# Rotated queries by SBUF copies, and two weight casts queued behind the exponentials, in a hybrid attention block

## The chip, the cores and the metric

The kernel runs on one core of a Trainium2 chip. The metric is the device time of one launch in microseconds (us). Three runs of the kernel before gave 628.59, 629.05 and 629.34 us; the median is 629.05.

## The reference

One decoder block over 512 tokens of width 1024, with 16 learned meta tokens in front (528 positions). Two attention branches of 16 heads each run side by side: MLA (queries and keys from low-rank projections, with a rotated part of 32 dimensions per head) and FoX (plain heads with a cumulative forget gate added to the logits). Both are gated, projected back and merged:

```python
u = rmsnorm(h, pre_norm_g)
cq, ckv, k_pe, z_mla, fq, fk, fv, f_logit, z_fox, gate_a, gate_b = split(u @ w_in)
q_m = concat(q_nope, rope(q_pe))          # from rmsnorm(cq) @ w_uq, per head 64 + 32
k_m = concat(k_nope, rope(k_pe))          # from rmsnorm(ckv) @ w_ukv; rope(k_pe) shared by the heads
o_mla = softmax(causal(q_m @ k_m.T * s)) @ v_mla
o_fox = softmax(causal(fq @ fk.T * s + cum_t - cum_s)) @ fv
y_mla = (o_mla * silu(z_mla)) @ w_br_mla ;  y_fox = (o_fox * silu(z_fox)) @ w_br_fox
out = h + rmsnorm((sigmoid(gate_a) * y_mla + sigmoid(gate_b) * y_fox) @ w_out)
```

All inputs and outputs are float32.

## The kernel before

Every float32 operand of a matmul is halved into a rounded part and a rest (`h` and `l` in the names: `wh`/`wl` for weights, `uTh`/`uTl` for activations), and each product is three matmuls: high by high, low by high, high by low. A block of weights of 128 columns is loaded as 512 KB into `wraw` (a pool of three buffers), cast to `wh` by ScalarE (ACT, line 126) and subtracted to `wl` by GpSimd (POOL, line 127 through the helper at line 101). A `unit` (line 171) is the list of matmul steps of one such block; its first step fetches the weights and issues the loads of the three blocks behind it.

After a front part (normalisation, transposition, small projections) come sixteen attention stages, for each pair of heads first FoX, then MLA: the first stage is FoX of pair 0, the second MLA of pair 0, the third FoX of pair 1. TensorE (PE) has an order written out by hand: in every stage the scores of the first three query blocks (`s0`, tile `st`), the value product of the stage before (`late`, tile `ov`, whose transposed probabilities are `pt`), the scores of the last query block (`s1`), and then the `fill`: projections that the next stages need. The second stage's fill is the projections of FoX pair 1: queries `fq`, half of the keys `fk`, values `v`, the other half of `fk`. A projection's result stands in one of three PSUM accumulators until ACT (`hlq`, `hlk`, line 238) and VectorE (DVE, line 101) have halved it; the second half of `v` needs the accumulator of `fq`.

The softmax of a stage: DVE masks and takes the minimum (line 642, `sf`), ACT takes the exponentials (line 650, six for the first three blocks of two heads, two for the last block), DVE sums and inverts (lines 658, 659, `su` and `ri`), POOL, ACT and DVE normalise into float16 halves `pn` (lines 664 to 678), and eight transposing DMAs put them into `pts` (tile `pt`, line 683).

The queues of ACT, DVE, POOL and of SyncE (SP), which issues all DMAs, are ordered by a planner that simulates the engines and issues what is ready first by priority. Two things bind it. `dma` (line 87) keeps a DMA in program order while `written[0]` is set, which holds for the first stage. And `wsplit` (line 121) queues its cast behind `behind[0]`, if there is one (`issue_after`: an order on the queue, without a semaphore). `behind` is filled in the first stage with the tanh of MLA's gate `z` (line 595) and cleared at the end of the second (line 788); so in the second stage the casts of `fq`, `fk` and `v` come behind that tanh.

The rotated queries: `pe_unit(0)` (line 483) computes them for heads 0 to 7; `rest` (line 517) adds and halves them on POOL into `rr[x]` (x = the first or second half of the rotation, inside `gT`), with 16 rows to each head, and stores them to `qpe_dram`: heads 0 and 1 at once (line 527, two DMAs for each x), heads 2 to 7 in the second stage (line 774). `load_qp` (line 461) loads the 128 rows of a pair into `QP`, for pair 0 in the first stage (line 763), ahead of that stage's transposes. The MLA scores read `QP`.

Of the kernel before, what the change touches and what calls it, by code (L numbers as in the profile page):

```python
# [16 lines left out]
AF = mybir.ActivationFunctionType  # L17
# [32 lines left out]
def f32(ap):  # L50
    return ap.bitcast(F32)
# [3 lines left out]
def block_kernel(ctx: ExitStack, tc: tile.TileContext, x, meta_tokens, pre_norm_g, w_in, fox_forget_b,  # L55
                 mla_q_norm_g, mla_kv_norm_g, w_uq, w_ukv, w_br_mla, w_br_fox, w_out, post_norm_g,
                 rope_tok, rope_pe, out):
    nc = tc.nc
# [23 lines left out]
    wp = ctx.enter_context(tc.tile_pool(name="wp", bufs=3))  # L82
    uid = [0]
    written = [False]
    behind, through, first_t = [], [], []

    def dma(out, src, start=None):

        ins = (start or nc.sync.dma_start)(out=out, in_=src)
        if written[0]:  # L90
            tc.keep_in_program_order(ins)
        return ins.ins

    def mm(*a, **k):
        nc.tensor.matmul(*a, **k)  # L95
# [4 lines left out]
    def split_lo(eng, lo, src, hi):  # L100
        eng.tensor_tensor(out=lo, in0=src, in1=f32(hi), op=ALU.subtract)  # L101
# [31 lines left out]
    def weights(srcs, wrap):  # L133

        st = {}

        def load():
            if "l" not in st:
                st["l"] = wload(srcs())

        def get():
            load()
            return wrap(wsplit(st["l"]))
        get.load = load
        return get
# [65 lines left out]
    def run(steps):  # L211
        for _, fn in steps:
            fn()
# [46 lines left out]
    with ExitStack() as ph:  # L260
# [30 lines left out]
        for c in range(4):  # L291
            r = pa.tile([128, 2, NSM], F32, tag="wsr", name=f"wsr{c}", bufs=4)
# [132 lines left out]
    with ExitStack() as att:  # L425
# [7 lines left out]
        QP = ac.tile([128, S], F32R, tag="QP", name="QP")  # L433
# [27 lines left out]
        def load_qp(pr):  # L461
            dma(f32(QP), qpe_dram[2 * pr : 2 * pr + 2].rearrange("h i x f s -> (h i x f) s"))
# [20 lines left out]
        def pe_unit(g):  # L483
            if g == 0:
                r0, tt = (p.rearrange("p a b -> p (a b)")[:, 0 : 8 * S].bitcast(F32).rearrange("p (c s) -> p c s", c=4)
                          for p in pts)
            else:
                r0, tt = gT[0][:, 4:8], gT[1][:, 4:8]
            rp = r0[:, 0:2]

            rr = [r0[:, 2:4], tt[:, 2:4]] if g else [t[:, 4:6] for t in gT]
            if g == 0:
                nc.sync.dma_start(rp, rope_pe)
            out = []
            w = {}

            def half(xi, ws=None):
                if ws:
                    w[0] = ws
                return (lambda k: w[0][2 * xi + k][0]), (lambda k: w[0][2 * xi + k][1])  # L500

            def srcs():
                if g:

                    tc.keep_in_program_order(nc.sync.dma_start(rp, rope_pe))
                return [wuqh[:, k, 8 * g : 8 * g + 8, NOPE + 16 * x : NOPE + 16 * x + 16]
                        for x in range(2) for k in range(2)]

            for xi in range(2):
                get = (lambda: half(1)) if xi else weights(srcs, lambda ws: half(0, ws))  # L510

                def done(i, ps, xi=xi):
                    for cs in range(2):
                        nc.vector.tensor_tensor(out=tt[:, 2 * xi + cs], in0=ps, in1=rp[:, cs], op=ALU.mult)
                out += unit(f"ppe{g}{xi}", get, cq_act, 2, REAL, done)

            def rest(x):

                nc.gpsimd.tensor_tensor(out=tt[:, x], in0=tt[:, x], in1=tt[:, 3 - x], op=(ALU.subtract, ALU.add)[x])
                hi, lo = rr[x][:, 0], rr[x][:, 1]  # L520
                nc.gpsimd.tensor_copy(hi.bitcast(F32R), tt[:, x])
                split_lo(nc.gpsimd, lo.bitcast(F32R), tt[:, x], hi)
                if g:
                    store(x, 0, 8)
                else:

                    store(x, 0, 2)

            def store(x, a, b):
                for i in range(2):  # L530
                    dma(qpe_dram[8 * g + a : 8 * g + b, i, x], rr[x][16 * a : 16 * b, i])
            return out, rest, store

        mw = {}
# [64 lines left out]
        def attention(br, pr):  # L599


            scale = (SC_MLA, SC_FOX)[br]
# [3 lines left out]
            def sets(h, b, c0, w):  # L606
                hs = slice(64 * h, 64 * h + 64)
                qs, ks = slice(128 * b, 128 * b + 128), slice(c0, c0 + w)
                out = [(q[hs, i, qs], k[hs, j, ks]) for i, j in ((0, 0), (1, 0), (0, 1))]
                if br:  # L610
                    return out + [(ONE[hs], CT[hs, ks])]
                return out + [(QP[hs, qs], KP[i][hs, ks]) for i in range(2)]

            sums, sfs = {}, {}

            def sf_of(h, b):
                o, n = SF_STEP * (b % 3), 144 + 128 * b
                return sfs[b // 3][:, h, o : o + n]

            def scores(g):  # L620

                banks = (((0, 0, 144, 0), (1, 0, 272, 144)), ((2, 0, 400, 0),)) if g == 0 else \
                    (((3, 0, HALF, 0),), ((3, HALF, L - HALF, 0),))

                def fn():
                    if g == 0:
                        for t in ("nb", "su", "ri"):
                            sums[t] = aw.tile([128, 2, 4], F32, tag=t, name=f"{t}{nm_}")
                    sfs[g] = aw.tile([128, 2, (2 * SF_STEP + 400, L)[g]], F32, tag=f"sf{g}", name=f"sf{nm_}{g}", bufs=1)
                    for ib, parts in enumerate(banks):  # L630
                        ps = [stp.tile([128, 512], F32, tag="st", name=f"st{nm_}{g}{ib}{h}") for h in range(2)]
                        for b, c0, w, o in parts:
                            for i, ops in enumerate(zip(*(sets(h, b, c0, w) for h in range(2)))):
                                for h, (Q, K) in enumerate(ops):
                                    mm(ps[h][:, o : o + w], Q, K, start=(i == 0), stop=(i == 4 - br))
                        for b, c0, w, o in parts:
                            m0 = 384 - 128 * b + c0
                            for h in range(2):
                                nb = sums["nb"][:, h, b : b + 1]

                                with tc.high_priority(offset=100):
                                    nc.vector.tensor_tensor_reduce(  # L642
                                        out=sf_of(h, b)[:, c0 : c0 + w], in0=ps[h][:, o : o + w],
                                        in1=maskt[:, m0 : m0 + w], scale=-scale, scalar=3.0e38 if c0 == 0 else nb,
                                        op0=ALU.add, op1=ALU.min, accum_out=nb)
                    with tc.high_priority(offset=60):
                        for b in GRP[g]:
                            for h in range(2):
                                sf = sf_of(h, b)
                                nc.scalar.activation(sf, sf, AF.Exp, bias=sums["nb"][:, h, b : b + 1], scale=-1.0,  # L650
                                                     accum_out=sums["su"][:, h, b : b + 1])
                return fn

            def norm(g):
# [71 lines left out]
        g = gate_unit()  # L726
# [3 lines left out]
        for si, (br, pr) in enumerate(stages):  # L730
# [10 lines left out]
            else:  # L741
                g = gate_unit()
# [9 lines left out]
        late = []  # L752
        for si, (br, pr) in enumerate(stages):
            s0, s1, n0, n1, va = attention(br, pr)

            for fn in [s0] + late + [s1]:
                fn()

            fill = fills[si]
            if si == 0:  # L760

                run(fill[:4])
                load_qp(0)
                n0()
                n1()
                first_t.extend(through)
                run(fill[4:])
            else:
                run(fill[:1])
                if si == 1:  # L770

                    written[0] = True
                    for x in range(2):
                        store0(x, 2, 8)
                    written[0] = False
                run(fill[1:5])
                n0()
                run(fill[5:12])
                n1()
                if 6 <= si < 8:  # L780

                    written[0] = True
                    rest1(si - 6)
                    written[0] = False
                run(fill[12:])
            written[0] = False
            if si == 1:
                behind.clear()
            late = [va]
# [146 lines left out]
```

## Time and profile before

| | us |
|---|---|
| median of three runs | 629.05 |
| the profiled execution's own time | 628.52 |
| its span, from first to last instruction | 626.7 |
| PE busy, share of the span | 602.4, 96% |
| ACT, DVE, POOL busy | 329.0, 310.4, 266.5 |
| mean granted TensorE clock | 0.996 of full speed |

The lines of the timeline give the start in us from the span's start, the duration in us, the engine, the line of the code, the operation with its output and inputs, the shapes, and how many instructions are merged; in brackets stands how long the engine was idle before it and what ended that. A row of waits names the engine that waited, for whom, and the total, the count and the longest. A row of the windows gives for a stretch the busy time and count of PE, of its weight loads, of DVE, ACT and POOL, and then the granted TensorE clock, the share of the DMA engines and GB/s. SPq is SyncE's queue of DMAs; its durations are times to issue, not to land.

### The profile page before, as it was taken

The page shows a single profiled execution, that of the slowest core. Times are in us where ns is not written, and L with a number is a line of the kernel's source. Part 1 is how long each engine was busy: PE and PEld are TensorE (multiplying, and loading weights), DVE is VectorE, ACT ScalarE, POOL GpSimd, SP SyncE. Part 2 cuts the span into 40 slices and gives each one's busy share as a digit, 9 for nine tenths or more (in the row PEclk, how much of TensorE's full clock was granted, in tenths as well). Part 3 has the DMA queues.
Part 4 walks back from the last instruction along what each step waited for, and adds up shares of the span by engine and source line. Part 5 has one row for each costly group of instructions (what it writes and reads, how often), then busy time and mean ns, then how long its engine had stood idle before and what let it go on. Part 6 is the DMA issues. An engine that isn't in the chain of part 4 may idle for free.

```text
span 626.7 us, 10961 instructions
## 1 busy us (share of the span) xinstructions
PE 602.4 (96%) x3810; PEld 507.7 (81%) x3810; DVE 310.4 (50%) x899; ACT 329.0 (52%) x738; POOL 266.5 (43%) x269
## 2 busy tenths in 40 slices
PE   3999998899999999999999999999999999999996
PEld 2879877788888889789888898887888888888885
DVE  4747753467566655764675666636321122023134
ACT  5747726567665665774685666657322222232321
POOL 3216715434344653444254433441744444444610
PEclk9999999899999999999999999999999999999999
DMA  9432369998978778878579586782433333333702
GB/s 286 106 101 51 73 150 191 210 178 169 183 167 152 166 170 169 193 177 198 126 163 189 136 165 163 171 164 67 135 102 100 88 90 92 100 102 114 256 33 101
DMA packets 223808, 90.10 MB, mean 144 GB/s; under 512 B 141628, under 2 KB 216764, under 8 KB 223752
## 3 DMA queue, kind: packets, MB, share of 16 engines
q1 hardware_dynamic: 223752, 89.39, 60.9%
q8 instruction: 30, 0.49, 0.3%
q14 instruction: 26, 0.21, 0.1%
HBM read 55.21 MB, written 4.26 MB: 95 GB/s over the span
## 4 chain that ended last, share of the span: by engine, by line
PE 86%; DVE 4%; ACT 3%; issue 2%; DMA 2%; SPq 1%; POOL 0%; DVEq 0%; ACTq 0%
PE pg L95 14%; PE py L95 14%; PE z L95 14%; PE v L95 9%; PE fk L95 7%; PE po L95 7%; PE fq L95 7%; PE st L95 4%; PE psm L95 3%; PE ov L95 3%; DVE sf L642 2%; ACT wh L126 2%; PE mq L95 2%; PE mk L95 1%; DMA wsr<-in_w_in_dram 1%
## 5 line engine op out<-in xcount | busy, mean ns | idle before, releaser
L101 POOL TENSOR_TENSOR wl<-wraw,wh 128x1024 fp32r<-128x1024 f32 (+1 forms) x90 | 208.4, 2319 | 223.4 <-ACT wh L126 218.6
L126 ACT CAST wh<-wraw 128x1024 fp32r<-128x1024 f32 (+1 forms) x90 | 89.9, 1001 | 175.4 <-PE v L95 48.5
L650 ACT ACTIVATE sf<-sf,nb 128x144 f32<-128x144 f32 (+3 forms) x128 | 72.0, 564 | 14.9 <-DVE nb L642 14.9
L678 DVE SCALAR_TENSOR_TENSOR pn<-sf,ri,pn 128x128 f16<-128x128 f32 (+3 forms) x128 | 66.0, 554 | 13.2 <-ACT pn L677 13.1
L677 ACT ACTIVATE pn<-sf,ri 128x128 f16<-128x128 f32 (+3 forms) x128 | 61.5, 551 | 19.2 <-ACT sf L650 18.5
L819 DVE SCALAR_TENSOR_TENSOR tb<-th,py 128x512 f32<-128x512 f32 x16 | 11.0, 686 | 101.9 <-PE py L95 101.9
L95 PE MATMUL st<-hlk,hlq 64*128 64x272 f32 (+3 forms) x480 | 52.5, 315 | 1.8 <-ACT hlk L238 0.6
L95 PE MATMUL z<-uTh,wh 128*128 128x512 f32 x128 | 50.9, 397 | 0.0
L95 PE MATMUL pg<-uTh,wh 128*128 128x512 f32 x128 | 50.2, 392 | 0.0
L95 PE MATMUL z<-uTh,wl 128*128 128x512 f32 x128 | 50.0, 391 | 0.0
L95 PE MATMUL z<-uTl,wh 128*128 128x512 f32 x128 | 49.9, 390 | 0.0
L95 PE MATMUL pg<-uTl,wh 128*128 128x512 f32 x128 | 49.8, 389 | 0.0
L95 PE MATMUL pg<-uTh,wl 128*128 128x512 f32 x128 | 49.8, 389 | 0.0
L95 PE MATMUL py<-gh,wl 128*128 128x512 f32 x128 | 49.8, 389 | 0.0
L95 PE MATMUL py<-gh,wh 128*128 128x512 f32 x128 | 49.8, 389 | 0.0
L95 PE MATMUL py<-gl,wh 128*128 128x512 f32 x128 | 49.8, 389 | 0.0
L642 DVE CUSTOM_DVE_ANT_0 sf<-st,maskt 128x272 f32<-128x272 f32 (+2 forms) x128 | 48.3, 433 | 0.8 <-PE st L95 0.8
L664 POOL TENSOR_TENSOR mt<-sf,ri 128x96 f32<-128x96 f32 (+1 forms) x32 | 9.5, 296 | 87.9 <-DVE ri L659 74.1
L95 PEld LDWEIGHTS st<-hlk,hlq 64*128 64x128 f32 x480 | 36.9, 185 | 11.9 <-DVE nb L642 2.7
L95 PE MATMUL v<-uTh,wh 128*128 128x256 f32 (+1 forms) x128 | 37.3, 291 | 3.0 <-DVE hlq L101 3.0
L95 PE MATMUL v<-uTl,wh 128*128 128x256 f32 (+1 forms) x128 | 37.2, 291 | 0.0
L95 PE MATMUL v<-uTh,wl 128*128 128x256 f32 (+1 forms) x128 | 37.1, 290 | 0.0
(182 smaller groups left out, 1404.2 us busy)
## 6 DMA issues: line engine op xcount, KB each, us to landing
wraw<-in_w_in_dram SPq DMA_DIRECT2D x56, 512.0 KB
wraw<-in_w_br_fox_dram SPq DMA_DIRECT2D x8, 512.0 KB
wraw<-in_w_br_mla_dram SPq DMA_DIRECT2D x8, 512.0 KB
wraw<-in_w_out_dram SPq DMA_DIRECT2D x8, 512.0 KB
QP<-qpe_dram SPq DMA_DIRECT2D x8, 256.0 KB
pt<-pn SPq DMA_TRANSPOSE x128
xr<-in_x_dram SPq DMA_DIRECT2D x4, 512.0 KB
out_dram<-yo SPq DMA_DIRECT2D x8, 256.0 KB
```

The lines of the kernel that those rows point to most:

```text
L95: nc.tensor.matmul(*a, **k)
L101: eng.tensor_tensor(out=lo, in0=src, in1=f32(hi), op=ALU.subtract)
L126: nc.scalar.copy(wh[:, :n], raw[:, :n])
L642: nc.vector.tensor_tensor_reduce(out=sf_of(h, b)[:, c0 : c0 + w], in0=ps[h][:, o : o + w], in1=maskt[:, m0 : m0 + w], scale=-scale, scalar ...
L650: nc.scalar.activation(sf, sf, AF.Exp, bias=sums["nb"][:, h, b : b + 1], scale=-1.0, accum_out=sums["su"][:, h, b : b + 1])
L664: nc.gpsimd.tensor_tensor(out=mt, in0=src, in1=ri.unsqueeze(3).broadcast_to([128, 2, nb_, META]), op=ALU.mult)
L677: nc.scalar.activation(hi, sf, AF.Copy, scale=rib)
L678: nc.vector.scalar_tensor_tensor(out=lo, in0=sf, scalar=rib, in1=hi, op0=ALU.mult, op1=ALU.subtract)
L819: nc.vector.scalar_tensor_tensor(out=tb[br], in0=ths[i, br], scalar=1.0, in1=py, op0=ALU.add, op1=ALU.mult)
```

## The change

The first pair's rotated queries no longer go through DRAM. In place of the four stores of heads 0 and 1 and the load of `QP`, `rest` issues eight DMAs from `rr[x]` straight into `QP`, one for each x, head and half, with 16 rows of 512 float32 (32 KB). The later pairs still go by `qpe_dram`.

The casts of weights that the second stage makes after its first fill steps (those of `fk` and `v`; the cast of `fq` is made within these first steps) are queued behind the last exponential of the first three query blocks of that stage, in place of the tanh.

```diff
-    behind, through, first_t = [], [], []
+    behind, through, first_t, exps = [], [], [], []
...
                 else:
-                    store(x, 0, 2)
+                    for h in range(2):
+                        for i in range(2):
+                            r = 64 * h + 32 * i + 16 * x
+                            dma(f32(QP[r : r + 16]), rr[x][16 * h : 16 * h + 16, i])
...
             sums, sfs = {}, {}
+            exps[:] = [None, None]
...
-                                nc.scalar.activation(sf, sf, AF.Exp, bias=sums["nb"][:, h, b : b + 1], scale=-1.0,
-                                                     accum_out=sums["su"][:, h, b : b + 1])
+                                exps[g] = nc.scalar.activation(sf, sf, AF.Exp, bias=sums["nb"][:, h, b : b + 1],
+                                                               scale=-1.0, accum_out=sums["su"][:, h, b : b + 1]).ins
...
             if si == 0:
                 run(fill[:4])
-                load_qp(0)
                 n0()
                 n1()
...
                 run(fill[1:5])
+                if si == 1:
+                    behind[:] = exps[:1]
                 n0()
                 run(fill[5:12])
```

## The prediction, on record before the result

> **What bounds the kernel now.** I read the page first, then who waits for whom on the engine that the page shows full, then the timeline of that engine where it waits, and from there the queues of the engines that it waits for.
>
> ```profile
> span 626.7 us, 10961 instructions
> PE 602.4 (96%) x3810; PEld 507.7 (81%) x3810; DVE 310.4 (50%) x899; ACT 329.0 (52%) x738; POOL 266.5 (43%) x269
> ```
> ```profile
> PE v L95 <- DVE hlq L101: 3.0, 1, 3.0
> ```
> TensorE (PE) is busy for 96% of the span, so only its stalls can be won. The longest one after the front stages is this single event. PE's timeline shows it, and smaller ones before it, all within the second attention stage (the brackets give the idle time before the row and what ended it).
>
> ```profile
> 88.87 0.56 PE L95 MATMUL st<-hlk,hlq 64*128 64x144 f32 x6
> ...
> 92.35 2.01 PE L95 MATMUL ov<-pt,vp 80*64 80x512 f16 x25 [0.78 <-DMA pt<-pn]
> ...
> 95.94 0.50 PE L95 MATMUL fq<-uTh,wh 128*128 128x512 f32 x1 [0.16 <-ACT wh L126]
> ...
> 98.37 0.50 PE L95 MATMUL fq<-uTh,wl 128*128 128x512 f32 x1 [1.69 <-POOL wl L101]
> ...
> 112.57 0.39 PE L95 MATMUL v<-uTh,wh 128*128 128x256 f32 x1 [2.99 <-DVE hlq L101]
> ...
> 120.00 0.56 PE L95 MATMUL st<-hlk,hlq 64*128 64x144 f32 x6
> ...
> 122.38 2.04 PE L95 MATMUL ov<-pt,vp 80*64 80x512 f16 x26
> ```
> ```profile
> 139.53 0.56 PE L95 MATMUL st<-hlk,hlq 64*128 64x144 f32 x6
> ...
> 145.65 0.50 PE L95 MATMUL fq<-uTh,wh 128*128 128x512 f32 x1
> ...
> 162.99 0.56 PE L95 MATMUL st<-hlk,hlq 64*128 64x144 f32 x6
> ```
> A stage runs from its first score matmul (st) to the next stage's. The second takes 120.00 - 88.87 = 31.13 us. The fourth, which has the same matmuls, takes 162.99 - 139.53 = 23.46 us. The difference, 7.67 us, is all that can be won here. It is more than the stalls, because after the 2.99 us stall the clock falls:
>
> ```profile
> 113.40:117.00 3.60, 3.60 (x20) 3.60 (x19) 0.00 (x0) 0.00 (x0) 0.36 (x1) 0.53 1.32 188
> 89.00:120.00 31.00, 25.37 (x196) 22.52 (x197) 14.13 (x48) 16.31 (x39) 12.93 (x14) 0.94 0.98 191
> ```
> The granted clock is 0.53 for 3.60 us, which loses 3.60 x 0.47 = 1.7 us. Together with 0.78 + 0.16 + 1.69 + 2.99 that is 7.3; the rest is restarts.
>
> Now the queue that feeds these stalls, SyncE's (SP):
>
> ```profile
> 68.41 2.24 SPq L89 DMA_TRANSPOSE vp<-vh  x1
> ...
> 71.51 2.70 SPq L89 DMA_DIRECT2D qpe_dram<-gT  x4
> 79.55 0.36 SPq L89 DMA_DIRECT2D QP<-qpe_dram  x1
> 80.01 10.59 SPq L89 DMA_TRANSPOSE pt<-pn  x8
> 91.06 1.98 SPq L89 DMA_DIRECT2D wraw<-in_w_in_dram  x3
> ...
> 94.96 2.63 SPq L89 DMA_TRANSPOSE vp<-vh  x1
> 97.64 3.97 SPq L89 DMA_DIRECT2D qpe_dram<-gT  x4
> 101.72 1.82 SPq L89 DMA_DIRECT2D wraw<-in_w_in_dram  x1
> ...
> 111.74 8.08 SPq L89 DMA_TRANSPOSE pt<-pn  x5
> ```
> The four stores are issued by 74.21. Then SP stands until 79.55, 5.34 us, because the load of QP needs them landed. Queued behind are the eight transposes (until 90.60) and the three loads at 91.06, the weights of fq, fk and v.
>
> ```profile
> 94.84 1.05 ACT L126 CAST wh<-wraw 128x1024 fp32r<-128x1024 f32 x1 [4.45 <-DMA wraw<-in_w_in_dram]
> ...
> 99.00 1.05 ACT L126 CAST wh<-wraw 128x1024 fp32r<-128x1024 f32 x1 [0.34 <-DMA wraw<-in_w_in_dram]
> 99.95 0.41 ACT L650 ACTIVATE sf<-sf,nb 128x144 f32<-128x144 f32 x1
> ...
> 111.22 0.57 ACT L238 CAST hlq<-fq 128x512 fp32r<-128x512 f32 x1
> ```
> ```profile
> 76.23 3.04 DVE L678 SCALAR_TENSOR_TENSOR pn<-sf,ri,pn 128x256 f16<-128x256 f32 x5 [0.50 <-ACT pn L677]
> ...
> 92.89 0.57 DVE L642 CUSTOM_DVE_ANT_0 sf<-st,maskt 128x400 f32<-128x400 f32 x1
> ...
> 103.12 0.39 DVE L658 TENSOR_SCALAR su<-su 128x6 f32<-128x6 f32 x1 [9.65 <-ACT sf L650]
> ...
> 111.82 0.69 DVE L101 TENSOR_TENSOR hlq<-fq,hlq 128x512 fp32r<-128x512 f32 x1 [0.61 <-ACT hlq L238]
> ```
> ```profile
> 95.97 2.34 POOL L101 TENSOR_TENSOR wl<-wraw,wh 128x1024 fp32r<-128x1024 f32 x1 [7.02 <-ACT wh L126]
> ...
> 103.88 0.35 POOL L664 TENSOR_TENSOR mt<-sf,ri 128x96 f32<-128x96 f32 x1 [0.40 <-DVE ri L659]
> ...
> 104.74 0.41 POOL L668 TENSOR_TENSOR pn<-mt,pn 128x96 f16<-128x96 f32 x1
> ```
> ScalarE (ACT) has the three casts ahead of the six exponentials, so the exponentials, whose last input was there at 93.46, wait for the third load and start at 99.95. VectorE stands 9.65 us behind them, and everything later shifts with it, down to hlq, whose accumulator the second half of v needs. So there are two causes: SP's wait makes the first cast late (fq stalls), and the order of ACT makes the softmax late (v stalls).
>
> **The change part by part.** First, the eight DMAs. No row shows a copy of 16 rows of 2 KB from SBUF to SBUF; the nearest are these:
>
> ```profile
> L407 SPq DMA_DIRECT2D CT<-ch x4: 497/584/650, 61.0 to 63.6; - x4
> ```
> ```profile
> L89 SPq DMA_DIRECT2D qpe_dram<-gT x4: 567/606/772, 71.5 to 73.6; - x4
> L89 SPq DMA_DIRECT2D QP<-qpe_dram x1: 357/357/357, 79.6 to 79.6; - x1
> ```
> An issue lies between 0.36 and 0.77 us; I take the stores' median, 0.61, as they have the same source, plus 0.03 to the next. Eight hold SP from 71.51 for 5.1 us, to 76.6 (bounds 74.6 and 77.9). The transposes can follow at once: the last of the inputs they read is finished at 79.27 and they take 1.32 us each, so none has to wait. They begin at 76.6 instead of 80.01: SP gains 3.4 us (2.1 to 5.4). QP itself is first read at about 89, over 12 us after its last issue; should it land later, every microsecond would be PE's.
>
> Shifted by 3.4, the last of these transposes is issued at 87.2. In the trace PE went on at 92.35, 1.75 us after the last issue ended; 87.2 + 1.75 lies before 91.16, where PE comes to ov, so 0.78 goes. The fq load lands so that its cast runs at 91.4, and GpSimd (POOL) has wl done 0.08 + 2.34 us after the cast ends, at 94.9. In the fourth stage fq begins 6.12 us after the stage (145.65), so here it can at 95.0, and its third matmul, the first to read wl, wants it at about 95.4. So 0.16 and 1.69 go too, with half a microsecond to spare; at the slow bound of the issues 0.8 us comes back.
>
> Second, the two later casts, of fk and v, go behind the first six exponentials. No semaphore is added: it is an order on ACT alone. The exponentials then start behind the first cast, at 92.5 instead of 99.95, and end 3.1 us later (VectorE's su, which needs them, ran at 103.12), at 95.6.
>
> ```profile
> 98.37 5.29 PE fq L95 x22
> 103.66 2.96 PE fk L95 x24
> ```
> The cast and the subtraction for fk end at 95.6 + 1.05 + 0.1 + 2.34 = 99.1. By these rows of the chain of waits PE wants them 5.29 us after 95.4, at 100.7, and those of v 2.96 later, at 103.6, where they are ready at 101.4. If POOL takes the normalisation's small operations first (103.88 to 105.15, 1.3 us), both are later by less than that, and still in time. The accumulator: from 99.95 to the hlq cast at 111.22 ACT took 11.3 us, now with 2.1 of casts in it, and DVE is done 1.3 later: 92.5 + 11.3 + 2.1 + 1.3 = 107.2. PE reached the stall 11.2 us after 98.37, so now at 106.6. A stall of 0 to 0.6 us stays; I book 0.3, since the casts fit partly into ACT's pauses. The clock then holds, and 1.7 goes with the 2.99. Queued behind the moved casts on ACT are the normalisation's copies and hlq, counted here.
>
> PE alone thus would gain 7.67 - 0.3 = 7.4 us. What is late next is SP: by the timeline it issues almost without pause from 91.06 to 119.82, when the last transpose of the second stage is out. With 1.75 for landing that is 121.57, 0.8 before ov at 122.38. PE can come forward by no more than SP does plus 0.8. SP comes forward by 3.4 plus what its own issues shorten. Between the first stage and the second the same kinds grew: vp 2.24 to 2.63, four stores 2.70 to 3.97, a load from 0.66 (a third of the row at 91.06) to 1.82, a transpose of pt from 1.32 to 1.62, which is 1.5 us for the five at 111.74. That is 4.3 us of stretch, in a time when the DMA share is 0.98. If none of it goes, PE gains 4.2 and waits at ov; if 3.2 goes, all 7.4. The same bytes still move in it, so I take 2.0, below the middle. **Sum**: 3.4 + 0.8 + 2.0 = 6.2 us, with 1.2 us of a new stall at the third stage's ov. Behind that PE has no stall that either edit touches. The profiled execution took 628.52 us, 0.53 under the median of 629.05; so it becomes 622.3, and the median 622.9.
>
> **The rivals.** *All of it hidden* (0.29): SP's stretch shrinks by 3.2 or more, ov does not wait, and the gain is 7.4: 621.6. For it: part of the stretch stands beside loads that waited for GpSimd, which now comes earlier. Against it: the DMA share of 0.98.
>
> *SP keeps its stretch* (0.16): gain 4.2, a stall of 3.2 us at the third stage's ov: 624.9. If the clock falls there as it did after 2.99 us, 1.7 more is lost: 626.6. The row shows that a stall of 2.99 us was enough, and that 1.69 us at 98.37 was not; I give the two halves of this rival the same chance. The Trainium skill (TensorE: Matmul & The Clock Gate, "What's actually happening") has the clock halve after at least one idle window of about 3.4 us, and come back after as long. The 3.60 us at 0.53 agree with the second part, but the 2.99 us stall undercuts the first. By the page this rival would keep its clock and end at 624.9; by the row 626.6.
>
> *The small DMAs cost what the wait cost* (0.08): at 1.0 us each, eight take as long as the stretch from 71.51 to 79.55, and SP gains nothing. Edit two alone then brings PE the slack of 0.8: 628.2, no change. Rows so far show at most 0.77. The Trainium skill (DMA: Bandwidth & Descriptors, "Rules for kernel authors") advises to coalesce many small transfers and calls those under 64 KB mostly overhead, which speaks for this rival; the 2.1 KB copies in 0.50 to 0.65 us bear out an overhead, not that it is larger.
>
> *Slower* (0.07): the casts fall not just behind the exponentials but behind the whole normalisation and hlq. Then fk's cast starts behind hlq, at 92.5 + 11.3 + 0.6 = 104.4 instead of 95.6, its wl is there at 107.9, PE stalls 7.2 us at fk and loses 1.7 to the clock: 8.9 against the 7.67 that could be won. With the second cast in front of fk's it is another 1.05, so 2.3 slower, 631.3. It decides from a start of fk's cast at 103.1 on. Against it: in the profile before, ACT's fixed order put all three casts ahead of the exponentials, so its planner has the loads landed by then, and would place the casts as soon as it may.
>
> **How the numbers follow.** The forecast, a gain between 5 and 7 us, has 0.40, with 622.1 to 624.1 as its own range. Faster by over 0.2% (1.3 us, about what a measurement here can tell) are the forecast, the first two rivals and nothing else: 0.85. The small-DMA rival gives no change, 0.08, and slower has 0.07. The range from 621.2 to 626.8 leaves out these last two and a sliver.
>
> **What would show it.** Right: no idle SP between the first stage's stores and transposes; eight issues of about 0.6 us from 71.5; fq's cast near 91.4; the exponentials directly behind it; the casts of fk and v behind the last of those six; no stall at fq or v; the clock at 1.00 throughout; a stall of about 1 us at the third stage's ov <- DMA pt. Wrong: exponentials still behind a cast that waits for its load, a stall at fk for wl, or a stall at the third stage's ov of 3 us and a low clock behind it.

## The result and the profile after

The changed kernel took 625.37 us (median of 4 runs, 624.62 to 625.72) against 628.96 us for the kernel before in the same measurement: a ratio of 0.9941, with a 95% interval from 0.9924 to 0.9959. Measured again later, the ratio was 0.9953 (0.9938 to 0.9969). The sign was forecast and the time lies in the range, but the gain is 3.6 us and not 6.2. The profiled execution took 625.12 us.

The page's first lines, and the longest waits of TensorE within the attention stages (total, count, longest):

```profile
span 623.3 us, 10966 instructions
PE 601.4 (96%) x3810; PEld 506.7 (81%) x3810; DVE 314.2 (50%) x899; ACT 328.8 (53%) x738; POOL 266.3 (43%) x269
```
```profile
PE v L95 <- DVE hlq L101: 2.2, 1, 2.2
...
PE st L95 <- ACT hlk L238: 1.2, 5, 0.5
...
PE fq L95 <- POOL wl L101: 0.6, 1, 0.6
```

PE is busy for about as long as before. The wait for hlq in v, which was to go, is still the longest. PE's timeline from the second stage into the third, with the waits in brackets:

```profile
88.62 0.56 PE L95 MATMUL st<-hlk,hlq 64*128 64x144 f32 x6
...
90.92 2.04 PE L95 MATMUL ov<-pt,vp 80*64 80x512 f16 x26
...
95.67 0.50 PE L95 MATMUL fq<-uTh,wl 128*128 128x512 f32 x1 [0.63 <-POOL wl L101]
...
109.02 0.58 PE L95 MATMUL v<-uTh,wh 128*128 128x256 f32 x1 [2.15 <-DVE hlq L101]
...
116.48 0.56 PE L95 MATMUL st<-hlk,hlq 64*128 64x144 f32 x6
...
118.23 0.91 PE L95 MATMUL st<-hlk,hlq 64*128 64x400 f32 x6 [0.53 <-ACT hlk L238]
...
119.25 2.04 PE L95 MATMUL ov<-pt,vp 80*64 80x512 f16 x26
```

The second stage takes 116.48 - 88.62 = 27.86 us instead of 31.13, so 3.27 of the 7.67 us are won. The stall of 0.78 at ov is gone, those at fq fell from 0.16 + 1.69 to 0.63, that at v from 2.99 to 2.15. The forecast stall at the third stage's ov (119.25) is not there. And the clock fell again behind v, as the windows show (the last three columns are granted clock, DMA share, GB/s):

```profile
89.00:116.50 27.50, 24.72 (x196) 21.99 (x194) 16.73 (x48) 15.87 (x37) 13.10 (x14) 0.94 0.97 185
109.00:112.50 3.50, 3.48 (x16) 3.48 (x17) 0.66 (x2) 0.00 (x0) 1.20 (x1) 0.51 0.97 115
```

At 0.51 for 3.50 us that loses 1.7 us, as much as before. SyncE's queue:

```profile
71.32 4.99 SPq L89 DMA_DIRECT2D QP<-gT  x8
76.42 11.11 SPq L89 DMA_TRANSPOSE pt<-pn  x8
87.58 2.58 SPq L89 DMA_DIRECT2D wraw<-in_w_in_dram  x3
...
94.60 3.94 SPq L89 DMA_DIRECT2D qpe_dram<-gT  x4
98.65 1.99 SPq L89 DMA_DIRECT2D wraw<-in_w_in_dram  x1
...
113.33 3.62 SPq L89 DMA_TRANSPOSE pt<-pn  x2
```

The eight DMAs are issued in 4.99 us (5.1 was forecast) and the transposes follow at 76.42 (76.6). But the last transpose of the second stage is out at 116.95, only 2.87 us earlier than 119.82; from the three loads on, SP needs 116.95 - 87.58 = 29.37 us where it needed 28.76. Now who made hlq late: ScalarE, VectorE and GpSimd between 92 and 109 us.

```profile
92.10 1.05 ACT L126 CAST wh<-wraw 128x1024 fp32r<-128x1024 f32 x1 [1.96 <-DMA wraw<-in_w_in_dram]
...
106.72 1.04 ACT L126 CAST wh<-wraw 128x1024 fp32r<-128x1024 f32 x1 [0.66 <-DMA wraw<-in_w_in_dram]
107.67 0.58 ACT L238 CAST hlq<-fq 128x512 fp32r<-128x512 f32 x1
```
```profile
98.84 1.92 DVE L682 SCALAR_TENSOR_TENSOR pn<-sf,ri,pn 128x256 f16<-128x256 f32 x1
...
101.49 2.87 DVE L682 SCALAR_TENSOR_TENSOR pn<-sf,ri,pn 128x256 f16<-128x256 f32 x3
...
108.28 0.69 DVE L101 TENSOR_TENSOR hlq<-fq,hlq 128x512 fp32r<-128x512 f32 x1 [1.39 <-ACT hlq L238]
```
```profile
98.01 5.00 POOL L101 TENSOR_TENSOR wl<-wraw,wh 128x1024 fp32r<-128x1024 f32 x2
```

Two things are new. The cast ahead of hlq (106.72, the third stage's first weights) waits for its load, which SP issued at 98.65, behind the four stores. And GpSimd's two subtractions, which the moved casts have shifted from beside the exponentials (98.73 to 103.48 before, when VectorE was waiting) into the normalisation, run beside VectorE's operations of line 682 (678 in the kernel before): 1.92 and 2.87 us for one and three of them, where the kernel before took 0.47 and 1.53. The row of three merges two shapes; one by one they take 1.81, 0.61 and 0.61 us, so it is the first two operations that are stretched, each beside one subtraction. My theory from here: hlq is late through these two, both consequences of the change and of a late SP; the stall then takes the clock with it. The rival is the prediction's: SP alone, by way of the transposes.

### The profile page after: what moved, and what is told of

The parts are those of the page before. It is cut to its first block, busy times and chain, and to the rows that moved or that the text cites. A ratio compares the mean times of both kernels' runs of the same rounds, so it can differ in the third digit from the quotient of the medians.

```text
span 623.3 us, 10966 instructions
## 1 busy us (share of the span) xinstructions
PE 601.4 (96%) x3810; PEld 506.7 (81%) x3810; DVE 314.2 (50%) x899; ACT 328.8 (53%) x738; POOL 266.3 (43%) x269
## 4 chain that ended last, share of the span: by engine, by line
PE 85%; DVE 4%; ACT 4%; DMA 2%; issue 2%; SPq 2%; POOL 0%; DVEq 0%; ACTq 0%
PE pg L95 14%; PE py L95 14%; PE z L95 14%; PE v L95 7%; PE po L95 7%; PE fk L95 7%; PE fq L95 7%; PE st L95 4%; PE psm L95 3%; PE ov L95 3%; DVE sf L646 2%; ACT wh L126 2%; PE mq L95 2%; DMA wraw<-in_w_in_dram 1%; SPq L89 1%
## 5 line engine op out<-in xcount | busy, mean ns | idle before, releaser
L682 DVE SCALAR_TENSOR_TENSOR pn<-sf,ri,pn 128x128 f16<-128x128 f32 (+3 forms) x128 | 68.6, 575 | 13.2 <-ACT pn L681 13.1
```

The source lines that it names most:

```text
L682: nc.vector.scalar_tensor_tensor(out=lo, in0=sf, scalar=rib, in1=hi, op0=ALU.mult, op1=ALU.subtract)
```

## The experiments

Stages are read from the starts of their first score matmuls, in us (one profiled execution of each kernel; the front part before the first stage varies by up to 1.9 us between executions of whatever kernel, so it is left out; in rows of variants the line numbers are up to three higher than in the changed kernel):

| kernel | ratio to before, 95% interval | second | third | fourth | fifth |
|---|---|---|---|---|---|
| before | 1 | 31.13 | 19.53 | 23.46 | 19.51 |
| changed kernel | 0.9941 (0.9924 to 0.9959) | 27.86 | 19.93 | 23.47 | 19.51 |
| changed kernel again | 0.9953 (0.9938 to 0.9969) | 27.75 | 20.29 | 23.45 | 19.53 |
| first edit alone | 0.9952 (0.9937 to 0.9967) | 28.45 | 19.53 | 23.45 | 19.54 |
| second edit alone | 1.0031 (1.0016 to 1.0046) | 28.58 | 22.04 | 23.46 | 19.52 |
| casts behind hlq | 0.9992 (0.9976 to 1.0008) | 24.86 | 25.51 | 23.47 | 19.54 |
| stores late | 1.0010 (0.9994 to 1.0026) | 25.42 | 19.51 | 30.58 | 19.54 |
| both of these | 0.9998 (0.9984 to 1.0012) | 24.92 | 19.54 | 28.98 | 19.54 |
| second pair direct too | 0.9976 (0.9963 to 0.9988) | 24.73 | 19.53 | 24.09 | 23.65 |
| subtractions in pieces | 0.9973 (0.9962 to 0.9984) | 27.76 | 19.64 | 23.48 | 19.54 |
| all of these | 1.0016 (1.0003 to 1.0029) | 23.97 | 20.75 | 24.80 | 22.70 |
| stores from GpSimd | 0.9918 (0.9902 to 0.9933) | 24.83 | 21.10 | 23.45 | 19.52 |
| that, casts behind hlq | 0.9930 (0.9907 to 0.9953) | 24.64 | 22.63 | 23.47 | 19.53 |
| first edit, stores from GpSimd | 1.0021 (1.0010 to 1.0033) | 31.75 | 19.52 | 23.47 | 19.54 |

**The edits one by one.** The first edit alone:

```diff
-                if si == 1:
-                    behind[:] = exps[:1]
```

> The first edit alone: eight DMAs from SBUF to SBUF, the casts of fk and v still behind the tanh. My theory: the queue of SyncE comes forward by 3.6 us as in the changed kernel, VectorE and GpSimd do not meet in the normalisation, and v still waits for hlq because the exponentials stand behind three casts; hlq comes at about 107.7 us, the stall at v is 1 to 1.5 us. About 625.2 us, so as good as both edits together, since the second edit gives back what it wins. Rival (the sum on record, where the second edit carries the stall at v): the stall at v stays near 3 us with the fall of the clock, 626.4 us.

Measured: 625.94 us, which lies between the two. PE still stalls for 2.55 us at v, and the clock falls. VectorE is not held, since GpSimd's subtractions come while it waits for the exponentials:

```profile
104.75 0.47 DVE L682 SCALAR_TENSOR_TENSOR pn<-sf,ri,pn 128x256 f16<-128x256 f32 x1
...
105.96 1.53 DVE L682 SCALAR_TENSOR_TENSOR pn<-sf,ri,pn 128x256 f16<-128x256 f32 x3
```

These are the durations of before (0.47, and 1.53 for three). So nearly the whole gain is the first edit's; the intervals of this kernel and of the changed one overlap. The second edit alone, with the way through DRAM kept:

```diff
-                    for h in range(2):
-                        for i in range(2):
-                            r = 64 * h + 32 * i + 16 * x
-                            dma(f32(QP[r : r + 16]), rr[x][16 * h : 16 * h + 16, i])
+                    store(x, 0, 2)
...
+                load_qp(0)
```

> The second edit alone; the queries of the first pair go through DRAM as before. My theory (VectorE is held by GpSimd's subtractions, and the third stage's first cast waits for its load ahead of hlq): the stalls at fq (0.16 and 1.69 us) stay, the stall at v shrinks from 2.99 to about 2.2 us, the clock still falls behind it, and the kernel takes about 628.1 us, 0.8 less than before. Rival (the sum on record, by which the second edit removes the 2.99 us at v and the 1.7 us of clock): no stall over 0.6 us at v, the clock holds, 624 to 625 us, or as far as SyncE lets it.

Measured: 0.3% slower than before, which neither theory had.

```profile
111.63 0.39 PE L95 MATMUL v<-uTh,wh 128*128 128x256 f32 x1 [2.23 <-DVE hlq L101]
...
121.45 0.91 PE L95 MATMUL st<-hlk,hlq 64*128 64x400 f32 x6 [2.67 <-ACT hlk L238]
```

The stalls at fq and v are as my theory had them (1.71 and 2.23). In this execution, one of the fastest of its kernel at 628.62 us with a mean clock of 0.999, the clock did not fall, and the second stage won 2.55 us. The third gave all but 0.04 of it back: hlk's cast stands behind a cast that waits 2.97 us for a load which SP, still late, has not brought. Of the other nine executions, all with a mean clock of 0.992 to 0.996, eight took 629.35 to 632.61 us; a fall of the clock on top would account for that, but only the one execution has a profile. So the second edit makes PE faster into a queue that cannot feed it.

**ScalarE's order alone.** In the changed kernel, the third stage's first casts behind hlq's:

```diff
+                cast = nc.scalar.copy(hl[:, 0, o : o + w_], ps).ins
+                if key == ("q", 1, 1):
+                    q1[:] = [cast]
...
             if si == 1:
-                behind.clear()
+                behind[:] = q1
+            elif si == 2:
+                behind.clear()
```

> The changed kernel, and the third stage's first casts of weights queued behind the cast of fq's result (hlq). My theory: hlq comes 1.6 us earlier, the stall at v falls from 2.15 to about 0.5 us and the clock holds, which brings TensorE forward by up to 3.4 us; but the last transpose of the second stage is issued at 117 us as before, so a stall of about 2.8 us appears at the third stage's ov, and at most 0.6 us is won: 624.8 us, or 626.5 if the clock falls behind that new stall. Rival (the stall at v is the only limit): 622.0 us and no stall at ov.

```profile
108.76 0.39 PE L95 MATMUL v<-uTh,wh 128*128 128x256 f32 x1 [0.70 <-DVE hlq L101]
...
119.50 1.37 PE L95 MATMUL st<-hlk,hlq 64*128 64x400 f32 x6 [3.59 <-ACT hlk L238]
```
```profile
118.13 1.04 ACT L126 CAST wh<-wraw 128x1024 fp32r<-128x1024 f32 x1 [3.62 <-DMA wraw<-in_w_in_dram]
119.08 0.37 ACT L238 CAST hlk<-fk 128x256 fp32r<-128x256 f32 x1
```

Measured: 628.76 us, which neither theory had. The stall at v falls to 0.70 and the clock holds: the second stage takes 24.86 us. The third takes 6 us more: ACT stands 3.62 us before a load, with hlk's cast behind it, and there the clock falls instead. The whole gain of the change is lost, 0.9992. SP is the next limit, as the prediction said, but its lateness reaches PE through the loads and ACT's order, not through the transposes and ov.

**SP's stores moved.** In the changed kernel, the four stores of heads 2 to 7 behind the second stage's last transposes:

```diff
-                if si == 1:
-                    written[0] = True
-                    for x in range(2):
-                        store0(x, 2, 8)
-                    written[0] = False
                 run(fill[1:5])
...
                 run(fill[5:12])
                 n1()
+                if si == 1:
+                    written[0] = True
+                    for x in range(2):
+                        store0(x, 2, 8)
+                    written[0] = False
```

> The changed kernel, with the four stores of heads 2 to 7 issued behind the second stage's transposes instead of ahead of them. My theory: the last transpose of that stage is issued about 4 us earlier (113 us), the load of the third stage's first weights lands earlier, so its cast does not wait (0.66 us less), but that cast still stands ahead of hlq and VectorE is still held in the normalisation: the stall at v is about 1.5 us. 624.7 us if the clock falls, 623 if it holds. Rival (SyncE's queue is the only limit): the stall at v stays at 2.1 us and the time at 625.3.

And both of these edits together:

> Both of these on top of the changed kernel: hlq first and the stores late. My theory (two limits one behind the other, hlq and SyncE's queue): neither a stall at v over 0.6 us nor one at the third stage's ov, the clock at full speed in the second stage: 3.4 us less than the changed kernel, 622.0 us. Rival (either of the two is enough): no better than the better of the two alone.

Measured: 629.09 us with the stores late, which neither theory had, and 628.49 with both edits, so no better than either alone; the rival had that, but not the reason. The stall at v falls to 1.39 and 0.67 us, the clock holds in the second stage in both, and with both edits the second and third stages together win 50.66 - 44.46 = 6.2 us. That this equals the gain forecast is chance, as it does not come by the forecast's steps. The fourth stage gives 5.52 us of it back (7.12 with the stores alone moved). SP's queue with both edits, and PE:

```profile
113.73 4.05 SPq L89 DMA_DIRECT2D qpe_dram<-gT  x4
117.89 1.80 SPq L89 DMA_DIRECT2D wraw<-in_w_in_dram  x1
123.63 0.35 SPq L89 DMA_DIRECT2D QP<-qpe_dram  x1
```
```profile
139.44 0.38 PE L95 MATMUL ov<-pt,vp 80*64 80x512 f16 x1 [3.01 <-DMA pt<-pn]
140.72 3.49 PE L95 MATMUL ov<-pt,vp 80*64 80x512 f16 x25 [0.91 <-DMA pt<-pn]
```

From 119.69 to 123.63 SP stands again, since the second pair's load waits for the stores: the very wait that the first edit had removed, two stages later. The transposes behind it come late, ov stalls, and the clock falls (25 ov matmuls in 3.49 us instead of 2.01).

**No stores in the second stage.** The second pair's queries by eight SBUF DMAs too, the rest of the stores behind the third stage's transposes, and the casts behind hlq:

```diff
+            def copy_qp(x, pr):
+                for h in range(2):
+                    for i in range(2):
+                        r, s = 64 * h + 32 * i + 16 * x, 32 * pr + 16 * h
+                        dma(f32(QP[r : r + 16]), rr[x][s : s + 16, i])
...
+            if pr == 1:
+                with tc.issue_after(second_t[0]):
+                    for x in range(2):
+                        qp_copy[0](x, 1)
+                return
```

> The changed kernel with two things more: the third stage's first casts are queued behind the cast of fq's hlq (as in the run before that did this alone), and the second pair's rotated queries also go from SBUF to SBUF in eight DMAs, behind the second stage's last transposes, so that the second stage issues no stores at all; the stores of the last two pairs' heads go behind the third stage's transposes. My theory (what is left of the stalls is SyncE's: stores, and a load that waits for them to land): second stage 24.9 us, third 19.5, fourth 23.5, no stall over 0.8 us, clock 1.00, about 622.6 us. Rival: the eight issues (5 us) ahead of the third stage's transposes make the fourth stage's ov wait 3 to 4 us, as the load of the queries did with the stores late: about 628 us.

Measured 626.20 us, 0.9976. The third stage is as my theory had it (19.53) and the fourth 0.6 us over (24.09), as the rival's stall there is 0.68 us and not 3 to 4. But the fifth takes 23.65 us: SP has hardly come forward there against the kernel before (its last transposes of the fourth stage are out at 161.65 against 160.68; counted from the first stage's start, 0.46 us earlier), so that PE, now ahead, stalls and loses the clock.

```profile
162.71 0.38 PE L96 MATMUL ov<-pt,vp 80*64 80x512 f16 x1 [1.59 <-DMA pt<-pn]
163.59 3.63 PE L96 MATMUL ov<-pt,vp 80*64 80x512 f16 x25 [0.50 <-DMA pt<-pn]
```

**VectorE beside GpSimd.** In the changed kernel, the subtractions of fk and v in four pieces:

```diff
-        split_lo(nc.gpsimd, wl[:, :n], raw[:, :n], wh[:, :n])
+        step = n // 4 if cut[0] else n
+        for o in range(0, n, step):
+            split_lo(nc.gpsimd, wl[:, o : o + step], raw[:, o : o + step], wh[:, o : o + step])
...
                     behind[:] = exps[:1]
+                    cut[0] = True
...
-            written[0] = False
+            written[0] = cut[0] = False
```

> The changed kernel, with GpSimd's subtractions for fk and v in the second stage cut from one instruction of 1024 columns into four of 256. My theory (a subtraction holds VectorE's operations with two SBUF inputs until it ends): the four operations of 128x256 at line 682 fall from 4.8 us together to about 2.9, but the cast of hlq still stands behind a cast that waits for its load (106.7 us), so the stall at v stays between 1.5 and 2.2 us: about 625.2 us, or 623.6 if the stall falls far enough to keep the clock. Rival (VectorE shares bandwidth with GpSimd for as long as it works, no lock): the four operations stay at 4.8 us together, time unchanged at 625.4.

```profile
99.43 0.93 DVE L685 SCALAR_TENSOR_TENSOR pn<-sf,ri,pn 128x256 f16<-128x256 f32 x1
...
101.09 2.87 DVE L685 SCALAR_TENSOR_TENSOR pn<-sf,ri,pn 128x256 f16<-128x256 f32 x3
```
```profile
98.60 6.65 POOL L102 TENSOR_TENSOR wl<-wraw,wh 128x256 fp32r<-128x256 f32 x8
```

The four operations take 3.80 us together: neither 2.9 nor 4.8. One by one they went from 1.92, 1.81, 0.61 and 0.61 us to 0.93, 0.85, 1.09 and 1.08. The first two now wait for a piece of 0.83 us (6.65 / 8) at most instead of for a whole subtraction of up to 2.45; the other two, which in the changed kernel came when GpSimd had finished (103.01), now meet pieces as well. That speaks for taking turns by whole instructions. The Trainium skill (SBUF — State Buffer, "Who interferes with whom") says so: a VectorE instruction with two SBUF inputs contends with a GpSimd instruction that reads SBUF, and that contention is an exclusive lock. The trace agrees: line 682 has two such inputs, sf and pn, while line 646, which takes its scores from PSUM, was not stretched (0.43 for 272 columns, before and after).

Of VectorE's 1.0 us, only 0.45 reach hlq: from the first exponential to hlq's cast, without the wait for the load, it is 13.51 us instead of 13.96. The sum `su` (line 662 of the changed kernel), 0.16 us there, now falls beside a piece and takes 0.70. And the cast ahead of hlq waits for its load for 1.39 us here instead of 0.66, so that the stall at v is 2.43, over the 1.5 to 2.2 of my theory. The kernel is no faster than the changed one: 0.9973 against 0.9941 and 0.9953, where the interval overlaps only the second. The pieces in the kernel with the second pair direct:

> The kernel with the second pair's rotated queries sent from SBUF to SBUF and the third stage's casts behind hlq, and GpSimd's subtractions in four pieces besides. My theory (VectorE's wait is the rest of the stall at v, 0.7 us): the stall at v goes, second stage 24.3 us, 622.0 us. Rival: the stall is set by ScalarE's order alone, no difference to the kernel without the pieces.

The stall at v falls to 0.3 us, where the prediction had booked it, and the second stage to 23.97. But 1.36 us came at the third stage's hlk, 1.06 at the fourth stage's ov and 2.27 + 0.49 at the fifth's, and the kernel is slower than before. So my figure of 622.0 missed by 7.5; why the later stalls are longer than without the pieces was not isolated.

**The stores on another queue.** This kernel differs from the changed one in the queue of the four stores alone; ACT, VectorE and PE issue the same instructions in the same order:

```diff
-                    dma(qpe_dram[8 * g + a : 8 * g + b, i, x], rr[x][16 * a : 16 * b, i])
+                    dma(qpe_dram[8 * g + a : 8 * g + b, i, x], rr[x][16 * a : 16 * b, i],
+                        None if g else nc.gpsimd.dma_start)
```

> The changed kernel with one edit: the four stores of heads 2 to 7 in the second stage are issued from GpSimd's queue instead of SyncE's; all other instructions of all engines stay in their order. GpSimd is idle from 88.9 to 93.2 us, where they fall. My theory (SyncE's issues are what is left: its 3.9 us of stores delay the load behind which the cast ahead of hlq waits): that load is issued 4 us earlier, the cast no longer waits, the stall at v falls from 2.15 to about 1.5 us, the clock does not fall (it did not after 1.39 and 1.69 us), the second stage takes 25.5 us instead of 27.9, and the kernel about 622.8 us, 2.4 less than the changed kernel beside it. Rival (the DMA engines, not SyncE, are the limit; the bytes are the same): the transposes and loads stretch by as much as SyncE saves, the load lands no earlier, and the time stays within 0.5 us of the changed kernel. Third case: GpSimd takes over a microsecond for an issue, and fq's wl comes late by the excess over 4.3 us.

Beside it on the same chip, the changed kernel:

> The changed kernel once more, on the same chip and beside the same runs of the kernel before as the two variants above, since the times of one kernel differ between chips by up to 0.8 us. Every theory: a ratio of 0.994 to the kernel before (0.9924 to 0.9959 as measured first).

Measured: 623.88 us, 0.9918, beside 626.40, 0.9953; the intervals do not overlap. GpSimd's row, SP's and ACT's:

```profile
88.47 2.58 POOL L89 DMA_DIRECT2D qpe_dram<-gT  x4
```
```profile
91.49 5.75 SPq L89 DMA_TRANSPOSE vp<-vh  x1
97.35 0.53 SPq L89 DMA_DIRECT2D wraw<-in_w_in_dram  x1
...
110.96 3.83 SPq L89 DMA_TRANSPOSE pt<-pn  x2
```
```profile
105.03 1.03 ACT L126 CAST wh<-wraw 128x1024 fp32r<-128x1024 f32 x1
105.97 0.57 ACT L238 CAST hlq<-fq 128x512 fp32r<-128x512 f32 x1
```
```profile
107.32 0.39 PE L95 MATMUL v<-uTh,wh 128*128 128x256 f32 x1 [1.36 <-DVE hlq L101]
...
116.20 0.91 PE L95 MATMUL st<-hlk,hlq 64*128 64x400 f32 x6 [1.71 <-ACT hlk L238]
```

The load is issued 1.3 us earlier and not 4: the transpose of vp beside the stores grew from 2.73 to 5.75 us (5.83 and 5.86 in the two other kernels with the stores on that queue, 2.26 to 3.10 in all eleven traces without), so the rival is right for three quarters of SP's saving. The 1.3 us are enough, because the cast ahead of hlq had to wait for only 0.66; it now starts without a wait, the stall falls to 1.36 and the clock holds. The second stage wins 6.3 us. The third gives 1.57 back at hlk, again behind a cast that waits for its load (2.04 us, at 114.83). So the 2.5 us against the changed kernel beside it, for the 2.4 of my theory, are in part luck: the second stage won more than it had, and the third lost what it did not have. The third stage's casts behind hlq on top of this:

> The kernel that queues the third stage's first casts behind the cast of hlq (0.9992 of the time before when it was run alone, because the next casts then waited for their loads and a stall of 3.6 us came in the third stage), now also with the four stores on GpSimd's queue. My theory: the loads come 4 us earlier, so the stall of 3.6 us in the third stage goes and only 0.7 us at v is left: second stage 24.9, third 19.5, fourth 23.5 us, about 622.2 us. Rival (DMA engines are the limit): the stall in the third stage stays over 2 us, about 627 to 628 us.

The stall of 3.59 us in the third stage fell to 1.63, under the rival's 2, so the stores on GpSimd's queue do relieve it; the second stage takes 24.64. Behind the 1.63 us the clock fell in the profiled execution (626.41 us, mean clock 0.996). Over all six executions the ratio of 0.9930 is not told apart from the 0.9918 without this edit. The two executions with a mean clock of 0.998 took 622.44 and 623.41, near the 622.2 forecast; the four with 0.996 took 624.51 to 626.69. Last, whether the second edit is of use once the stores are off SP:

> The first edit alone, with the four stores of the second stage issued from GpSimd's queue; the casts of fk and v stand ahead of the exponentials, as before. (SyncE's queue comes out in another order too: the loads of the third stage and that of the queries stand ahead of the transposes.) My theory (both things are needed: the second edit is worth nothing while SyncE is late, and something when it is not): the exponentials still start behind the third cast, the stall at v stays at about 2.5 us and the clock falls behind it in most executions: about 0.995 of the time before, like the first edit alone, against 0.992 with the second edit and GpSimd's stores. Rival (the second edit is worth nothing at all, SyncE was everything): 0.992.

```profile
100.35 1.05 ACT L126 CAST wh<-wraw 128x1024 fp32r<-128x1024 f32 x1 [5.21 <-DMA wraw<-in_w_in_dram]
```
```profile
113.70 0.58 PE L95 MATMUL v<-uTh,wh 128*128 128x256 f32 x1 [6.35 <-DVE hlq L101]
```

Slower than before, at 1.0021, and worse than either theory: the stores are now issued among the three loads (88.00 to 90.70), the third load lands late, and its cast waits 5.21 us with all six exponentials behind it. That the stores hold this load back is likely, but was not isolated. With the second edit the same casts stand behind the exponentials and wait for nothing. So the second edit, worth nothing measurable while SP issues the stores, decides between 0.9918 and 1.0021 when GpSimd does. SP's order differs here too, so that not all of the 1% need be the casts.

## Why the prediction was right in sign and range, and wrong in size

**The eight DMAs**: right. 4.99 us for 5.1, transposes at 76.42 for 76.6, no stall at ov. The three loads began at 87.58, as the shift of 3.4 us had it, but fq's cast began 4.52 us behind that instead of 3.78 (91.06 to 94.84), at 92.10 and not 91.4, so 0.63 us at fq stayed. The 0.8 that the prediction allowed there stood for slow issues, which did not come; that it covers the 0.63 is luck.

**The moved casts**: exponentials from 93.05 on for 92.5, none of fk's and v's casts late: right. The rival by which they would fall behind the normalisation did not come.

**"DVE is done 1.3 later: ... 107.2"**: this step failed. It was done at 108.28 + 0.69 = 108.97. From the first exponential to hlq's cast went 14.62 us, not 11.3 + 2.1 = 13.4. The 11.3 came from a trace in which GpSimd's subtractions lay ahead of the normalisation and the load of the next stage's weights had long landed. Moved and made earlier, the chain met both. With 0.55 from the late start and 1.22 from these (0.66 for the load; the other 0.56 is near the 0.45 that the pieces gave back), less 0.27 because PE came later (106.87 for 106.6), the 0.6 became 2.1; measured were 2.15. The ladder of runs gives the shares: 2.15 as changed, 1.36 without the wait for the load, 0.65 with the cast itself behind hlq as well; and 0.3 in the kernel that takes VectorE's stretch apart too. That last rung is another kernel, so its share is less sure.

**"The clock then holds, and 1.7 goes with the 2.99"**: failed with the step before it. A stall of 0 to 0.6 us would have kept the clock, as the runs with 0.65 to 0.70 show; 2.15 did not. These 1.7 us and the 1.85 of the longer stall make up 3.5 of the 4.1 us between the 7.4 forecast for PE and the 3.27 measured; 0.63 at fq is the rest. In the profiled execution's own time, 628.52 to 625.12, the 3.27 us of the second stage lose 0.40 in the third (hlk) and gain 0.25 in the front part; 0.28 are spread behind.

**"SP comes forward 3.4 + 2.0"**: mis-sized. It came forward by 2.87. Of its stretch nothing went; SP's own stretch from the loads on even grew by 0.6. The first half of the rival "SP keeps its stretch" was right on this, and its 624.9 is nearer to 625.37 than my 622.9. Its place was wrong, and mine too: there is no stall at the third stage's ov in the changed kernel, nor with the stores on GpSimd's queue, where PE reaches ov at 117.23 and the last transpose is out at 114.79. SP's lateness goes through the weight loads into ACT's fixed order, ahead of hlq and hlk.

**The small DMAs** cost less than their rival needed: 0.62 us each, not 1.0.

## What to carry to other kernels

When a change moves a step to a new place, price the steps around it there: take its neighbours' durations and the landing of every load queued in the same order from the new time, not from the old trace. An engine with a fixed order passes on the lateness of one load to all that stands behind it, so the next bound may show at another tile than the one whose DMA is late. And a queue that is issued without a pause shifts a wait rather than losing it: of the six kernels that won over 6 us in the second stage, the four with all stores on SP's queue gave 4.8 to 6.0 of them back one to three stages later, the two with stores on GpSimd's queue 1.6 and 3.1.

## What the runs showed of the hardware

The clock: a stall's length alone does not decide. It fell to half after single stalls of 2.99, 2.55, 2.43, 2.19 and 2.15 us, and after 1.63 us in one kernel; it did not after 2.23 and 2.67 us (second edit alone), nor after 1.71, 1.39 and 0.7.

The traces show what does decide. In all fourteen the clock changes only at whole multiples of 3.413 us after its first rise, which comes 16.65 to 20.16 us into the span; it stays low for one such window, or for two behind the longest stalls (3.45, 3.59 and 6.35 us). Cut into these windows, the traces have the clock halved behind every window in which PE is idle for 2.02 us or more, behind none with up to 1.57, and in between behind 1.63 but not behind 1.69, 1.71, 1.80 and 1.81. The 2.99 us of the kernel before left 2.43 in one window; the 2.23 of the second edit alone left 1.80, and its 2.67 fell into two windows as 1.29 and 1.38. So a stall of 2 to 3 us costs 1.7 us more or nothing more, as the windows happen to fall, and that differs between executions (in the two traces of the changed kernel the first rise lies 50.80 and 50.17 us ahead of the first stage).

The Trainium skill (TensorE: Matmul & The Clock Gate, "What's actually happening") has a free-running window of about 3.4 us and lets the clock halve after at least one idle one. The traces agree on the window; but one that was idle for 2.02 of its 3.41 us was enough here.

Issuing four stores took 2.58 us on GpSimd's queue and 3.94 on SP's at the same bytes; the transpose of vp beside them was stretched instead, from 2.73 to 5.75 us.
